# Order of work at five changes of stage in a one-core decoder layer: final scaling of the first token half, the mixer's second weights, the delta rule outputs' loads, the decays' product, the state banks

## The chip, the core and the metric

The kernel runs on one core of a Trainium2 chip. TensorE (PE in the rows) multiplies, VectorE (DVE), ScalarE (ACT) and GpSimd (POOL) work on tiles, and SyncE (SP) issues the transfers between device memory and the core's memory. Each engine takes its own instructions in the order in which they were written into its program. The metric is the time of one execution in microseconds (us).

## The reference: one layer of two feed-forward blocks around a mixer

1024 tokens of width 1024 pass through one layer: half a SwiGLU block (hidden width 2816), a mixer that runs a gated delta rule (8 heads) and a Mamba-2 state-space scan (16 heads) on one combined projection, another half SwiGLU block, and a last RMS norm. All is float32.

```python
def rms_norm(x, w):
    xf = x.astype(jnp.float32)
    y = xf * lax.rsqrt(jnp.mean(xf * xf, axis=-1, keepdims=True) + EPS)
    return (y * w.astype(jnp.float32)).astype(x.dtype)

def swiglu(h, w_gate, w_up, w_down):
    a = jnp.einsum("bld,df->blf", h, w_gate)
    b = jnp.einsum("bld,df->blf", h, w_up)
    return jnp.einsum("blf,fd->bld", jax.nn.silu(a) * b, w_down)
...
def hybrid_mixer(h, w_in, ...):
    proj = jnp.einsum("bld,de->ble", h, w_in).astype(jnp.float32)
    ...
    o = gated_delta_rule(q, k, v, g, beta)          # 8 heads of 128
    o = rms_norm(o, gdn_norm_w) * jax.nn.silu(gdn_z.reshape(bsz, seqlen, GDN_HEADS, GDN_HEAD_DIM))
    ...
    y = ssd_scan(xs, dt, a_neg, b, c)               # 16 heads of 64, 2 groups
    y = y + xs * ssm_d[:, None]
    y = y.reshape(bsz, seqlen, SSM_W) * jax.nn.silu(ssm_z)
    ...
    mixed = jnp.concatenate([o_gdn, o_ssm], axis=-1).astype(h.dtype)
    return jnp.einsum("ble,ed->bld", mixed, w_out)

def reference(x, ...):
    x = x + 0.5 * swiglu(rms_norm(x, ffn1_norm[i]), ffn1_w_gate[i], ffn1_w_up[i], ffn1_w_down[i])
    x = x + hybrid_mixer(rms_norm(x, mix_norm[i]), w_in[i], ...)
    x = x + 0.5 * swiglu(rms_norm(x, ffn2_norm[i]), ffn2_w_gate[i], ffn2_w_up[i], ffn2_w_down[i])
    return rms_norm(x, final_norm)
```

## The kernel before

Each float32 operand is split into two parts, a rounded one and the rest: ACT casts (`A.copy`, the high part), and DVE subtracts the cast from the source (the low part). A product is then three matmuls of 128x128 by 128x512 (high by high, high by low, low by high; `mm3` and `product`). So every weight tile goes through a load (SP), a cast (ACT) and a subtraction (DVE) before TensorE can use it, and the order of these in the three queues decides when it is ready. Python code is written stage by stage; a scheduler places each stage's instructions by its own priorities, and within an engine the order is then fixed. `tc.issue_after(x)` keeps what is written under it behind the instruction x.

The stages in order: ffn1 (gate and up products, then the down products, each by a seven-product scheme on 512x512 blocks), the mixer's projections and the four units of the state-space scan (`un` 0 to 3), the eight delta-rule heads, the output projection with `w_out`, ffn2, and the final norm. The change touches five places where one stage hands over to the next.

**The mixer's first products (lines 629 to 660, 732).** The last down product of ffn1 finishes its four token blocks of the second half one by one. `norm_second` squares them, makes `rstd` and the scaled rows `xn` (one on ACT, L645, one on DVE, L646), and `norm_ht` lets TensorE transpose them (L196), eight times four blocks; ACT writes `hhi` (L213) and DVE `hlo` (L214). The projection weights come by `next_w`, which hands out a ready pair `whi`, `wlo` and starts the next: one load `wst`, two casts L136, two subtractions L137.

**The state-space units (lines 801 to 950).** A unit transposes its inputs four times into the two buffers of the PSUM tag `mx` (L844); DVE reads each bank twice, for `xdt` and `xe` (L849, eight instructions). `state()` makes seven of the running states: one product of `xe` and `bn` into the one bank of the tag `oo` (L858), four multiplications on ACT (L865), one addition on DVE that frees the bank (L867). `decays(b)` loads a broadcast row into `md`, and makes `cte` (one exponential on ACT, one product on DVE, L878) and `md` (a mask on POOL, eight exponentials on ACT, L884, one product with `cbt` on DVE, L886). Then the outputs come in two batches of 128x128 products (L899); a batch starts only when both of its `md` are made and its states are there:

```python
first = inter(1, 1, 0)
tc.add_manual_dep(first.ins, pairs[1][4].ins.name, ..., reason="one run of products")
```

**The delta rule's outputs (lines 955 to 975, 1243 to 1290).** Each head stores its output `vr` and its gate to device memory (`mix_scr`, `z_scr`). In the output projection `out_prep` takes a pair of heads: it loads `nat` (the outputs, 1 MB) and `zg` (the gates, two loads), both in the ring of weight tiles `wst`; TensorE transposes `nat` (L965), DVE scales by the gate (`hd`, L968), ACT and DVE split into `mtt` (L970, L971). There are four such preparations: two for the pairs of `n = 0`, two for those of `n = 1`. The loads of the weights `w_out` (`out_w`) use the ring too.

**The end of ffn2 (lines 438 to 510, 1309 to 1352).** The last of the seven down products (`m == 7`) has six steps, numbered 0 to 5 here; step 5 is half as wide. For each step `dn.prep` loads two weight blocks `wst` and the hidden rows `hraw`, DVE adds the blocks (L450), and ACT and DVE split both (`hid` and `wd`, L218 and L219). Steps 2 to 5 are multiplied bank by bank, so TensorE needs the weights of steps 2 to 5 within the first of four token blocks. After the sixth product (`m == 6`) the first token half is complete, and `finish_first` squares it (L164), makes `rstd` (eleven short DVE instructions) and scales the four blocks by `rstd` and the norm's weights (L1321), with a store behind each.

## Time and profile before

| | us |
|---|---|
| median of 3 runs (lowest to highest) | 2347.31 (2346.55 to 2348.21) |
| the profiled execution, its own time | 2346.0 |
| its span, first to last instruction | 2344.0 |
| TensorE busy | 2288.8 (98%) |
| VectorE busy | 1726.0 (74%) |
| ScalarE busy | 1100.7 (47%) |
| mean granted TensorE clock | 0.997 |

The span is read against TensorE's busy time: what is left, 55.2 us, are its idle stretches. A row of the timeline gives the start, the duration, engine, line, operation and tiles, and in square brackets the idle time of that engine before it with what ended it.

### The profile page before, as it was taken

What the parts mean: (1) busy time and instruction counts of PE and PEld (TensorE: products, weight loads), DVE (VectorE), ACT (ScalarE), POOL (GpSimd) and SP (SyncE); (2) the same over time, 40 slices, a digit from 0 to 9 for tenths busy, and PEclk for the clock granted to TensorE, in tenths of its full rate; (3) what the DMA queues carried; (4) which work ended last, traced back from release to release, by engine and by line L of the source; (5) the groups of instructions that cost most, each with busy time, mean ns of one, the idle gap of its engine ahead of it and who ended that gap; (6) DMA issues with size and microseconds to landing.
All of it is one profiled execution on the core that took longest, in us unless ns stands there. A gap on an engine that the chain in (4) does not pass through costs nothing.

```text
span 2344.0 us, 31560 instructions
## 1 busy us (share of the span) xinstructions
PE 2288.8 (98%) x11798; PEld 1873.4 (80%) x11798; DVE 1726.0 (74%) x3332; ACT 1100.7 (47%) x1996; POOL 52.8 (2%) x117
## 2 busy tenths in 40 slices
PE   6999999999999999999999999999999999999997
PEld 4788888888878878788888888787878888888886
DVE  7877777667765675668778878777697777766787
ACT  7433333343357775773455555422553333334334
POOL 0000000000000110000000000000000000000000
PEclk9999999999999999999999999999999999999999
DMA  2332333474652222232332222326222333329445
GB/s 110 108 113 95 108 103 113 160 289 130 220 179 74 90 90 60 68 93 64 82 82 73 80 82 65 109 66 255 90 86 97 108 108 111 108 92 343 147 155 196
DMA packets 220968, 281.33 MB, mean 120 GB/s; under 512 B 46906, under 2 KB 153591, under 8 KB 219791
## 3 DMA queue, kind: packets, MB, share of 16 engines
q1 hardware_dynamic: 220814, 279.33, 36.4%
q8 instruction: 92, 1.51, 0.3%
q14 instruction: 62, 0.50, 0.1%
HBM read 211.55 MB, written 67.73 MB: 119 GB/s over the span
## 4 chain that ended last, share of the span: by engine, by line
PE 79%; DVE 7%; issue 6%; ACT 5%; DMA 2%; POOL 1%; SPq 0%; DVEq 0%; POOLq 0%; ACTq 0%
PE ps_pj L121 8%; PE ps_pj L123 8%; PE ps_pj L122 8%; PE ps_pj L314 6%; PE ps_pj L313 6%; PE ps_pj L315 6%; PE ps_mx L313 3%; PE ps_mx L314 3%; PE ps_mx L315 3%; PE ps_pj L472 2%; PE ps_pj L473 2%; PE ps_pj L471 2%; PE ps_oo L313 2%; PE ps_oo L314 2%; PE ps_oo L315 2%
## 5 line engine op out<-in xcount | busy, mean ns | idle before, releaser
L121 PE MATMUL ps_pj<-hhi,whi 128*128 128x512 f32 x832 | 335.5, 403 | 0.0
L123 PE MATMUL ps_pj<-hhi,wlo 128*128 128x512 f32 x832 | 333.2, 400 | 0.0
L122 PE MATMUL ps_pj<-hlo,whi 128*128 128x512 f32 x832 | 332.9, 400 | 0.0
L314 PE MATMUL ps_pj<-bl,ah 128*128 128x512 f32 x704 | 274.9, 391 | 1.9 <-DVE bl L219 1.9
L313 PE MATMUL ps_pj<-bh,ah 128*128 128x512 f32 x704 | 274.6, 391 | 1.9 <-ACT sg L373 0.9
L315 PE MATMUL ps_pj<-bh,al 128*128 128x512 f32 x704 | 274.1, 390 | 0.0
L121 PEld LDWEIGHTS ps_pj<-hhi,whi 128*128 128x128 f32 x832 | 157.0, 189 | 28.8 <-issue 0.7
L123 PEld LDWEIGHTS ps_pj<-hhi,wlo 128*128 128x128 f32 x832 | 157.0, 189 | 28.5
L122 PEld LDWEIGHTS ps_pj<-hlo,whi 128*128 128x128 f32 x832 | 157.0, 189 | 27.7
L313 PEld LDWEIGHTS ps_pj<-bh,ah 128*128 128x128 f32 x704 | 131.8, 188 | 32.7 <-ACT bh L218 2.5
L218 ACT CAST ah<-wst 128x512 fp32r<-128x512 f32 x88 | 54.7, 623 | 219.2 <-PE ps_oo L314 137.8
L314 PEld LDWEIGHTS ps_pj<-bl,ah 128*128 128x128 f32 x704 | 132.2, 188 | 31.4 <-DVE bl L219 4.7
L315 PEld LDWEIGHTS ps_pj<-bh,al 128*128 128x128 f32 x704 | 132.2, 188 | 27.2
L218 ACT CAST hid<-hraw 128x1024 fp32r<-128x1024 f32 (+1 forms) x84 | 82.1, 980 | 146.5 <-PE ps_oo L473 55.8
L292 DVE TENSOR_TENSOR as<-wst 128x512 f32<-128x512 f32 x220 | 145.0, 684 | 1.6 <-DMA wst<-in_ffn_w_up_dram 1.5
L219 DVE TENSOR_TENSOR al<-as,ah 128x512 fp32r<-128x512 f32 x220 | 140.2, 684 | 4.3 <-ACT ah L218 4.3
L313 PE MATMUL ps_mx<-bh,ah 128*128 128x512 f32 x352 | 137.5, 393 | 0.9 <-ACT bh L218 0.7
L314 PE MATMUL ps_mx<-bl,ah 128*128 128x512 f32 x352 | 138.0, 392 | 0.2 <-DVE bl L219 0.2
L315 PE MATMUL ps_mx<-bh,al 128*128 128x512 f32 x352 | 137.4, 390 | 0.0
L218 ACT CAST ah<-as 128x512 fp32r<-128x512 f32 x220 | 124.2, 617 | 14.3 <-DVE as L292 14.1
L219 DVE TENSOR_TENSOR hid<-hraw,hid 128x1024 fp32r<-128x1024 f32 x84 | 95.0, 1132 | 35.3 <-ACT hid L218 34.6
L219 DVE TENSOR_TENSOR al<-wst,ah 128x512 fp32r<-128x512 f32 x88 | 60.6, 690 | 74.0 <-ACT ah L218 73.9
(412 smaller groups left out, 5094.3 us busy)
## 6 DMA issues: line engine op xcount, KB each, us to landing
hraw<-hid_scr SPq DMA_DIRECT2D x70, 512.0 KB, 4.0
hid_scr<-hs SPq DMA_DIRECT2D x110, 256.0 KB, 2.2
wst<-in_ffn_w_down_dram SPq DMA_DIRECT2D x50, 512.0 KB, 4.3
wst<-in_ffn_w_gate_dram SPq DMA_DIRECT2D x22, 1024.0 KB, 5.4
wst<-in_ffn_w_up_dram SPq DMA_DIRECT2D x22, 1024.0 KB, 5.2
wst<-in_w_in_dram SPq DMA_DIRECT2D x36, 512.0 KB, 5.3
hid_scr<-sg SPq DMA_DIRECT2D x44, 256.0 KB, 2.0
keep<-in_ffn_w_down_dram SPq DMA_DIRECT2D x20, 512.0 KB, 7.6
```

The costliest lines, as they stand in the source:

```text
L121: T.matmul(o, lhsT=wh, rhs=mh, start=first, stop=False)
L122: T.matmul(o, lhsT=wh, rhs=ml, start=False, stop=False)
L123: T.matmul(o, lhsT=wl, rhs=mh, start=False, stop=last)
L218: A.copy(out=hi, in_=src)
L219: V.tensor_tensor(out=lo, in0=src, in1=hi.bitcast(F32), op=ALU.subtract)
L292: V.tensor_tensor(out=t, in0=v[0], in1=v[1], op=v[2])
L313: T.matmul(bank, lhsT=wh[:, k], rhs=bh[:, k], start=a, stop=False, skip_group_check=True)
L314: T.matmul(bank, lhsT=wh[:, k], rhs=bl[:, k], start=False, stop=False, skip_group_check=True)
L315: T.matmul(bank, lhsT=wl[:, k], rhs=bh[:, k], start=False, stop=z, skip_group_check=True)
L471: T.matmul(bank, lhsT=hh, rhs=wh, start=first and k == 0, stop=False, skip_group_check=True)
L472: T.matmul(bank, lhsT=hh, rhs=wl, start=False, stop=False, skip_group_check=True)
L473: m = T.matmul(bank, lhsT=hl, rhs=wh, start=False, stop=last and k == n - 1, skip_group_check=True)
```

## The change

Five edits, all on the order of work or on where it is buffered; no arithmetic is added or removed.

1. `finish_first` keeps the squares and `rstd`; the four scalings with their stores, and the parts of the second token half that were called `early`, move into `between()`. It is handed to `down_all` as the hook that runs when the last step of `m == 7` has been prepared.
2. `norm_ht` returns its last ACT instruction, and the mixer's first `next_w()` (the second weights) is placed behind it with `issue_after`.
3. `out_prep` is cut in two, `out_load` and the rest. `nat` and `zg` leave the ring `wst` for a pool `natp` of their own with one buffer each. The first pair's loads are written two blocks into `n == 1`, the second pair's behind the first preparation, ahead of the weights `out_w`.
4. The product of `md` with `cbt` is placed behind the unit's last `xe`.
5. `state()` uses the tags `oo` and `mx` in turn.

```diff
--- before.py
+++ after.py
@@ -210,9 +210,10 @@
         ts = slice(half * 512, (half + 1) * 512)
         for k in range(NK):
             pt = transposed(xns, k)
-            A.mul(out=hsl(hhi, k, ts), in_=pt, mul=wcol[:, k:k + 1])
+            m = A.mul(out=hsl(hhi, k, ts), in_=pt, mul=wcol[:, k:k + 1])
             V.scalar_tensor_tensor(out=hsl(hlo, k, ts), in0=pt, scalar=wcol[:, k:k + 1],
                                    in1=hsl(hhi, k, ts).bitcast(F32), op0=ALU.mult, op1=ALU.subtract)
+        return m
 
     def split(hi, lo, src):
         A.copy(out=hi, in_=src)
@@ -646,7 +647,7 @@
             V.tensor_scalar(out=xn[:, 1], in0=xt[4 + i], scalar1=r[:, 1:2], scalar2=None, op0=ALU.mult)
             xns.extend((xn[:, 0], xn[:, 1]))
             if i == 3:
-                norm_ht(1, xns, nrm[1], *h2)
+                h2.append(norm_ht(1, xns, nrm[1], *h2))
 
         def before_last():
             load_gates_w()
@@ -654,7 +655,7 @@
 
         with tc.tile_pool(name="dtmp0", bufs=1, reuse_waits="tile") as dtmp:
             down_all(dtmp, xt, x_v, dn, [before_last], norm_first, lambda i: square(i, 1), norm_second)
-        hhi, hlo = h2
+        hhi, hlo, last_h = h2
 
     cm = ExitStack()
     gp = cm.enter_context(tc.tile_pool(name="gates", bufs=1, reuse_waits="tile"))
@@ -729,7 +730,9 @@
                 T.matmul(p[0:64], lhsT=gw[:, k], rhs=hsl(hlo, k, ts), start=False, stop=(k == NK - 1))
             A.copy(out=gsb[:, ts], in_=p[0:64])
 
-        wa = next_w()
+
+        with tc.issue_after(last_h.ins):
+            wa = next_w()
         bt = gp.tile([P, L], F32, name="bt", tag="xst", bufs=2)
         conv_silu(s1, wa, 0, cw_s, 8, bt, bias=cb_s[:, 8:9], between=gate_proj)
         pt = psum("mx")
@@ -846,7 +849,8 @@
             ptv = pt.rearrange("p (i h c) -> p i h c", i=2, h=4)
             for name, lst, sc in (("xdt", xdts, bc2(dtn, b0)), ("xe", xes, bc2(dxe, b0))):
                 t = s1.tile([P, 2, 256], F32, name=name, tag=name, bufs=4)
-                V.tensor_tensor(out=t.rearrange("p i (h c) -> p i h c", h=4), in0=ptv, in1=sc, op=ALU.mult)
+                last_x = V.tensor_tensor(out=t.rearrange("p i (h c) -> p i h c", h=4), in0=ptv, in1=sc,
+                                         op=ALU.mult)
                 lst.append(t)
 
 
@@ -854,7 +858,7 @@
 
         def state():
             b = len(sts) - 1
-            p3 = psum("oo")
+            p3 = psum(("oo", "mx")[b % 2])
             T.matmul(p3[:, 0:256], lhsT=bn[:, b], rhs=xes[b // 2][:, b % 2], start=True, stop=True)
             sn = s2p.tile([P, 256], F32, name="sn2", bufs=6)
             if b == 0:
@@ -883,8 +887,9 @@
                 for j in range(2):
                     A.activation(out=md[:, i, j], in_=md[:, i, j], func=AF.Exp,
                                  bias=ngc[:, b + j, hh:hh + 1])
-            made = V.tensor_tensor(out=md, in0=md,
-                                   in1=cbt[:, b:b + 2].unsqueeze(1).to_broadcast([P, 4, 2, P]), op=ALU.mult)
+            with tc.issue_after(last_x.ins):
+                made = V.tensor_tensor(out=md, in0=md, in1=cbt[:, b:b + 2].unsqueeze(1)
+                                       .to_broadcast([P, 4, 2, P]), op=ALU.mult)
             return md, cte, made
 
 
@@ -952,12 +957,15 @@
 
     pools = []
 
-    def out_prep(grp, mh, ml):
-        nat = wp.tile([P, NB, 256], F32, name="nat", tag="wst")
+    def out_load(grp):
+        nat = natp.tile([P, NB, 256], F32, name="nat")
         nc.sync.dma_start(out=nat, in_=mix_scr[grp])
-        zg = wp.tile([P, 2, L], F32, name="zg", tag="wst")
+        zg = natp.tile([P, 2, L], F32, name="zg")
         for j in range(2):
             nc.sync.dma_start(out=zg[:, j], in_=z_scr[2 * grp + j])
+        return nat, zg
+
+    def out_prep(nat, zg, mh, ml):
         for j in range(2):
             for half in range(2):
                 pt = psum("mx")
@@ -995,6 +1003,8 @@
         ready0.append(group_prep(0))
 
 
+    cn = ExitStack()
+    natp = cn.enter_context(tc.tile_pool(name="natp", bufs=1, side="right", reuse_waits="tile"))
     with ExitStack() as cg:
         g1 = cg.enter_context(tc.tile_pool(name="gdn1", bufs=1, reuse_waits="tile"))
         g2 = cg.enter_context(tc.tile_pool(name="gdn2", bufs=2, reuse_waits="tile"))
@@ -1240,13 +1250,13 @@
         else:
             V.scalar_tensor_tensor(out=o, in0=p, scalar=r, in1=o, op0=ALU.mult, op1=ALU.add)
 
-    def pair_prep(n, g, ms):
+    def pair_prep(n, g, ms, loaded=None):
 
         if n == 0:
             m = mtt[2 * g:2 * g + 2]
         else:
             m = [hbp[0].tile([P, 2, L], F32R, name="mt2", tag=f"b{2 * g + i}") for i in range(2)]
-        out_prep(2 * n + g, *m)
+        out_prep(*(loaded or out_load(2 * n + g)), *m)
         ms.append(m)
 
     def pair_tile(b, dh, w, ms, o):
@@ -1269,12 +1279,15 @@
 
             if b == 2 and n < 3:
                 ready = group_prep(n + 1)
+                if n == 1:
+                    loaded = out_load(0)
             elif b == 2:
+                pair_prep(0, 0, ms[0], loaded)
+                loaded = out_load(1)
                 wa = out_w(0, 0)
-                pair_prep(0, 0, ms[0])
             for dh in range(2):
                 group_tile(n, b, dh, *cur)
-    pair_prep(0, 1, ms[0])
+    pair_prep(0, 1, ms[0], loaded)
     wb = out_w(0, 1)
     for b in range(NB):
         nc.sync.dma_start(out=xt2[b], in_=x_scr[:, b])
@@ -1302,6 +1315,7 @@
     x1 = normalise(1, npool, xt2, jtag="h7")
     b_second(npool, x0, x1, nrm[2], H)
     c2.close()
+    cn.close()
 
 
     dn = gate_up_phase(1, npool, H, ffn2_w_gate[0], ffn2_w_up[0], ffn2_w_down[0], raws, ops)
@@ -1317,10 +1331,7 @@
         nc.sync.dma_start(out=wrow, in_=final_norm.partition_broadcast(P))
         junk = npool.tile([P, D], BF16, name="junk", tag="q")
         r = rms_stats(npool, xt2, 0, 4, junk)
-        for b in range(4):
-            V.scalar_tensor_tensor(out=xt2[b], in0=xt2[b], scalar=r[:, b:b + 1], in1=wrow,
-                                   op0=ALU.mult, op1=ALU.mult)
-            nc.sync.dma_start(out=out_v[:, b], in_=xt2[b])
+        rows.append(r)
 
     def part(i, dh):
 
@@ -1329,11 +1340,16 @@
         A.activation(out=junk, in_=xt2[4 + i][:, ds], func=AF.Square, accum_out=ss[:, 4 * dh + i:4 * dh + i + 1])
         V.tensor_tensor(out=xw[i // 2][:, i % 2, ds], in0=xt2[4 + i][:, ds], in1=rows[0][:, ds], op=ALU.mult)
 
-    def early(i):
-        part(i, 1)
-        if i == 3:
-            V.tensor_scalar(out=ss[:, 4:8], in0=ss[:, 4:8], scalar1=1.0 / D, scalar2=EPS,
-                            op0=ALU.mult, op1=ALU.add)
+    def between():
+
+        for b in range(4):
+            V.scalar_tensor_tensor(out=xt2[b], in0=xt2[b], scalar=rows[1][:, b:b + 1], in1=rows[0],
+                                   op0=ALU.mult, op1=ALU.mult)
+            nc.sync.dma_start(out=out_v[:, b], in_=xt2[b])
+        for i in range(4):
+            part(i, 1)
+        V.tensor_scalar(out=ss[:, 4:8], in0=ss[:, 4:8], scalar1=1.0 / D, scalar2=EPS,
+                        op0=ALU.mult, op1=ALU.add)
 
     def finish(i):
         part(i, 0)
@@ -1349,7 +1365,7 @@
             nc.sync.dma_start(out=out_v[:, 4 + i, dh * 512:(dh + 1) * 512], in_=o[:, dh * 512:(dh + 1) * 512])
 
     with tc.tile_pool(name="dtmp1", bufs=1, reuse_waits="tile") as dtmp:
-        down_all(dtmp, xt2, x_scr, dn, [], finish_first, early, finish)
+        down_all(dtmp, xt2, x_scr, dn, [between], finish_first, lambda i: None, finish)
 
 
 NAMES = ["x", "ffn1_norm", "ffn1_w_gate", "ffn1_w_up", "ffn1_w_down", "mix_norm", "w_in",
```

On ACT, at the mixer's first products (`xn`: scaled rows of the second token half, `whi`: high part of the mixer's second weights, `hhi`: high part of the transposed rows). Before:

```order
L631 ACTIVATE junk,ss_3721<-xtb 128x512 x3
L645 ACTIVATE xn<-xtb,rstd 128x1024
L136 CAST whi<-wst 128x8x128
L645 ACTIVATE xn<-xtb,rstd 128x1024
L136 CAST whi<-wst 128x8x128
L213 ACTIVATE hhi<-ps_sc,cols 128x512 x4
```

After:

```order
L632 ACTIVATE junk,ss_3721<-xtb 128x512 x3
L646 ACTIVATE xn<-xtb,rstd 128x1024 x2
L213 ACTIVATE hhi<-ps_sc,cols 128x512 x5
L770 ACT_TABLE_LOAD
L770 ACTIVATE alog<-alog 128x24
L213 ACTIVATE hhi<-ps_sc,cols 128x512 x3
L136 CAST whi<-wst 128x8x128 x2
```

The two casts of the weights stood around the second `xn`; they now stand behind the eighth `hhi`, and the two `xn` follow each other.

On DVE, at the start of unit 1's outputs (`md`: decays times `cbt`, `xdt` and `xe`: scaled inputs that free the transposes' banks, `sn`: states, `wlo`: low part of projection weights). Before:

```order
L886 TENSOR_TENSOR md<-md,cbt 128x1024
L878 TENSOR_TENSOR cte<-cte,ct 128x1024
L886 TENSOR_TENSOR md<-md,cbt 128x1024
L849 TENSOR_TENSOR xdt<-ps_mx,dtn 128x512
L849 TENSOR_TENSOR xe<-ps_mx,dxe 128x512
L849 TENSOR_TENSOR xdt<-ps_mx,dtn 128x512
L849 TENSOR_TENSOR xe<-ps_mx,dxe 128x512
L849 TENSOR_TENSOR xdt<-ps_mx,dtn 128x512
L849 TENSOR_TENSOR xe<-ps_mx,dxe 128x512
L849 TENSOR_TENSOR xdt<-ps_mx,dtn 128x512
L849 TENSOR_TENSOR xe<-ps_mx,dxe 128x512
L861 COPY sn_6436<-ps_oo 128x256
```

After:

```order
L882 TENSOR_TENSOR cte<-cte,ct 128x1024
L852 TENSOR_TENSOR xdt<-ps_mx,dtn 128x512
L852 TENSOR_TENSOR xe<-ps_mx,dxe 128x512
L852 TENSOR_TENSOR xdt<-ps_mx,dtn 128x512
L852 TENSOR_TENSOR xe<-ps_mx,dxe 128x512
L852 TENSOR_TENSOR xdt<-ps_mx,dtn 128x512
L852 TENSOR_TENSOR xe<-ps_mx,dxe 128x512
L852 TENSOR_TENSOR xdt<-ps_mx,dtn 128x512
L852 TENSOR_TENSOR xe<-ps_mx,dxe 128x512
L865 COPY sn_6436<-ps_oo 128x256
L891 TENSOR_TENSOR md<-md,cbt 128x1024 x2
L871 TENSOR_TENSOR sn_6440<-ps_mx,sn_6440 128x256
```

Both products of `md` stood ahead of the first `xdt`; they now stand behind the first state, and the second state reads a bank of `mx`.

On DVE, in the last down product of ffn2 (`wst`: sum of two weight blocks, `wd`: their low part, `hid`: low part of the hidden rows, 128x1024 in steps 3 and 4, 128x512 in step 5). Before, from the four scalings through the weights of step 3 (the first `wd`), step 4 and step 5 to the first addition of the second token half:

```order
L1321 SCALAR_TENSOR_TENSOR xt2b<-xt2b,rstd,wrow 128x1024 x4
L219 TENSOR_TENSOR wd<-wst,wd 128x1024
L450 TENSOR_TENSOR wst<-wst 128x1024
L219 TENSOR_TENSOR hid<-hraw,hid 128x1024
L219 TENSOR_TENSOR hid<-hraw,hid 128x512
L219 TENSOR_TENSOR wd<-wst,wd 128x1024
L450 TENSOR_TENSOR wst<-wst 128x512
L219 TENSOR_TENSOR wd<-wst,wd 128x512
L477 SCALAR_TENSOR_TENSOR xt2b<-ps_pj,xt2b 128x512
```

After, beginning behind the split of step 3's weights with the sum of step 4's:

```order
L451 TENSOR_TENSOR wst<-wst 128x1024
L117 TENSOR_TENSOR rs_t<-rs_t,rstd 128x4
L1351 TENSOR_SCALAR ss_18312<-ss_18312 128x4
L118 SCALAR_TENSOR_TENSOR rstd<-rs_t,rstd 128x4
L1346 SCALAR_TENSOR_TENSOR xt2b<-xt2b,rstd,wrow 128x1024
L220 TENSOR_TENSOR hid<-hraw,hid 128x1024
L220 TENSOR_TENSOR wd<-wst,wd 128x1024
L451 TENSOR_TENSOR wst<-wst 128x512
L1346 SCALAR_TENSOR_TENSOR xt2b<-xt2b,rstd,wrow 128x1024
L220 TENSOR_TENSOR wd<-wst,wd 128x512
L1346 SCALAR_TENSOR_TENSOR xt2b<-xt2b,rstd,wrow 128x1024 x2
L478 SCALAR_TENSOR_TENSOR xt2b<-ps_pj,xt2b 128x512
```

The four scalings stood in one run ahead of the split of step 3's weights; they now stand behind it, one ahead of step 4's split, one ahead of step 5's, and two behind that.

## Rows read from the trace of the kernel before

**Rows 1.** The page's first part: busy us, share and instructions of each engine.

```profile
PE 2288.8 (98%) x11798; PEld 1873.4 (80%) x11798; DVE 1726.0 (74%) x3332; ACT 1100.7 (47%) x1996; POOL 52.8 (2%) x117
```

**Rows 2.** Waits of PE: line, waited for; us in all, times, longest.

```profile
PE ps_pj L472 <- DVE wd L219: 5.1, 4, 3.2
PE ps_mx L844 <- DVE xe L849: 3.6, 2, 1.8
PE ps_oo L858 <- DVE sn L867: 2.9, 4, 0.8
```

**Rows 3.** Windows: us, busy of PE, PEld, DVE, ACT, POOL; granted clock, DMA share, GB/s.

```profile
686.80:690.20 3.40, 3.40 (x11) 2.55 (x10) 2.13 (x3) 0.72 (x2) 0.00 (x0) 0.50 0.50 121
1594.80:1598.20 3.40, 3.40 (x12) 2.66 (x11) 3.34 (x6) 1.96 (x4) 0.00 (x0) 0.50 0.29 91
2304.05:2311.53 7.48, 7.48 (x35) 6.20 (x33) 6.40 (x17) 5.06 (x9) 0.00 (x0) 1.00 0.50 164
2315.00:2318.40 3.40, 3.00 (x6) 1.77 (x6) 3.40 (x5) 1.05 (x1) 0.00 (x0) 0.50 0.96 314
```

**Rows 4.** Timeline of ACT, DVE, PE at the mixer's first products.

```profile
683.33 1.04 ACT L136 CAST whi<-wst 128x1024 fp32r<-128x1024 f32 x1 [3.65 <-DMA wst<-in_w_in_dram]
684.27 1.15 ACT L645 ACTIVATE xn<-xtb,rstd 128x1024 f32<-128x1024 f32 x1
...
681.04 0.75 DVE L646 TENSOR_SCALAR xn<-xtb,rstd 128x1024 f32<-128x1024 f32 x1
...
685.48 0.65 PE L196 MATMUL ps_sc<-ident,xn 128*128 128x128 f32 x4 [2.79 <-ACT xn L645]
```

**Rows 5.** Timeline of DVE and PE in state-space unit 1.

```profile
822.22 1.23 DVE L886 TENSOR_TENSOR md<-md,cbt 128x1024 f32<-128x1024 f32 x1 [6.88 <-ACT md L884]
...
833.32 0.42 DVE L867 TENSOR_TENSOR sn<-ps_oo,sn 128x256 f32<-128x256 f32 x1 [2.15 <-ACT sn L865]
...
847.22 1.23 DVE L886 TENSOR_TENSOR md<-md,cbt 128x1024 f32<-128x1024 f32 x1 [0.82 <-ACT md L884]
...
824.79 0.63 PE L844 MATMUL ps_mx<-ident,xs 128*128 128x128 f32 x4 [1.82 <-DVE xe L849]
```

**Rows 6.** Timeline of SP, DVE, PE at the second output preparation.

```profile
1585.96 0.32 SPq L957 DMA_DIRECT2D nat<-mix_scr  x1
...
1593.51 1.41 DVE L968 SCALAR_TENSOR_TENSOR hd<-ps_mx,cols,zg 128x512 f32<-128x512 f32 x2 [3.82 <-DMA zg<-z_scr]
...
1592.28 1.06 PE L965 MATMUL ps_mx<-ident,nat 128*128 128x128 f32 x8 [1.58 <-DMA nat<-mix_scr]
1594.32 0.74 PE L965 MATMUL ps_mx<-ident,nat 128*128 128x128 f32 x4 [0.97 <-DVE hd L968]
```

**Rows 7.** Timeline of PE in the last down product.

```profile
2311.53 0.39 PE L471 MATMUL ps_pj<-wd,hid 128*128 128x512 f32 x1
2315.12 0.79 PE L472 MATMUL ps_pj<-wd,hid 128*128 128x512 f32 x1 [3.21 <-DVE wd L219]
...
2319.12 0.50 PE L472 MATMUL ps_pj<-wd,hid 128*128 128x512 f32 x1 [1.00 <-DVE wd L219]
...
2321.21 0.50 PE L472 MATMUL ps_pj<-wd,hid 128*128 128x512 f32 x1 [0.22 <-DVE wd L219]
```

**Rows 8.** Timeline of DVE and ACT in the last down product.

```profile
2300.98 1.22 DVE L219 TENSOR_TENSOR wd<-wst,wd 128x1024 fp32r<-128x1024 f32 x1
...
2304.85 0.17 DVE L166 TENSOR_SCALAR ssv<-ss 128x4 f32<-128x4 f32 x1 [1.52 <-ACT junk L164]
...
2309.06 4.87 DVE L1321 SCALAR_TENSOR_TENSOR xt2b<-xt2b,rstd,wrow 128x1024 f32<-128x1024 f32 x4
2313.85 1.22 DVE L219 TENSOR_TENSOR wd<-wst,wd 128x1024 fp32r<-128x1024 f32 x1
...
2316.23 1.05 ACT L218 CAST wd<-wst 128x1024 fp32r<-128x1024 f32 x1 [3.97 <-DVE wst L450]
```

**Rows 9.** The page's sixth part: transfers, count, KB each, us to landing.

```profile
wst<-in_ffn_w_down_dram SPq DMA_DIRECT2D x50, 512.0 KB, 4.3
```

## Prediction

> **What bounds the kernel now.** The first part of the page comes first: TensorE is busy for 2288.8 us [rows 1], and the span is 2344.0 us, so all that an order of work can win is in 55.2 us of idle time, plus what a lowered clock costs. No step here takes a product away. The table of what TensorE waits for comes next. Three of its rows belong to the places that are edited: the weights of the down product, 5.1 us, of which 0.6 lie elsewhere, as the three waits of the last product add up to 3.21 + 1.00 + 0.22 = 4.43 [rows 2, 7]; the `mx` banks behind `xe`, 3.6 us in two waits; the `oo` bank behind `sn`, 2.9 us in four [rows 2]. The timeline adds 2.79 us before the transposes of `xn` [rows 4] and 1.58 and 0.97 us at the second output preparation [rows 6]. The third view is the granted clock: three stretches of 3.40 us stand at 0.50, which is 1.2 GHz, and each begins right behind one of these waits, 686.8 behind the 2.79, 1594.8 behind the 1.58 and 0.97, 2315.0 behind the 3.21 [rows 3, 4, 6, 7]. At half speed 3.40 us of products give 1.7 us of work at full speed, so each such stretch costs 1.7 us. The waits of 1.8 us in the state-space units have no such stretch behind them. In all the places hold 4.43 + 3.6 + 2.9 + 2.79 + 2.55 + 3 x 1.7 = 21.4 us, 0.9% of the time. That is the ceiling.
>
> **The mixer's second weights.** ACT runs in order. It had the cast of `whi` ahead of the second ACT `xn`, and the cast waited for its load to 683.33; `xn` ran at 684.27 and TensorE's transposes at 685.48 [rows 4]. The same `rstd` was ready at 681.04, where DVE made its own `xn` [rows 4]. With the casts behind the last `hhi`, `xn` can start at 681.04 and end at 681.04 + 1.15 = 682.19. TensorE stood there from 685.48 - 2.79 = 682.69 [rows 4], so the wait goes whole, and with it the stretch at 0.50: 2.79 + 1.7 = 4.49. What is late next: the casts and the two DVE subtractions behind them now run after eight evictions. These weights serve the projection behind the gates and the first B and C columns, so many products lie between. The load behind them starts later as its ring slot is freed later; I take 0.5 for a small wait in the chain of eight evictions, whose banks ACT and DVE free in turn. **Gain 4.0, bounds 2.5 and 4.8** (the lower one if one wait of half the old length, 1.4, comes back without the slow clock and 0.6 behind it; the upper adds 0.3 of earlier evictions).
>
> **The decays' product and the state banks.** In unit 1 DVE waited 6.88 us, to 822.22, for the last exponential of `md`, though the transposes to be read stood ready; the bank came free late and TensorE waited 1.82 us [rows 5]. Behind `xe`, the product no longer holds DVE: the eight reads take as long as before, but begin about 2 us sooner, so TensorE's third transposes find their bank. That happens in units 1 and 3: 3.6 us [rows 2]. The four waits on the single `oo` bank, 2.9 us, of which 0.3 at the longest is jitter in my reading, go where the next state has another bank. What takes their place: the two products of `md`, 1.23 us each [rows 5], now stand between the first state and the second. By my walk through DVE's new order in unit 1, the third state, which the first batch needs, ends at 831.9 instead of 833.32 + 0.42 = 833.74 [rows 5], and TensorE comes for it at about 832.0; that is nearly no margin. For the second batch the last `md` product ended at 847.22 + 1.23 = 848.45 [rows 5]; ACT reaches its exponentials 1.8 to 2 us sooner, so 846.3 to 846.6, where TensorE comes at about 846.2 to 846.8. So of 6.5 I take 5.0, losing 0.2 in each of eight batches. **Gain 5.0, bounds 1.5 and 6.5** (the lower one: only the 3.6 is gained and 0.26 per batch lost).
>
> **The delta rule's outputs.** Only the first pair's loads come early. The second pair's share one buffer with them: `nat` waits for the first preparation's transposes, which is what released it at 1585.96 before too [rows 6], so the transfer lands about where it did, at 1592.28 [rows 6], perhaps 0.9 us sooner as the first eight transposes no longer alternate with products. In front of the second `hd`, DVE now has four splits of `w_out`, 1.16 to 1.22 us each by the nearest row, a split of the same 128x1024 shape [rows 8]: 4.7 us, against a gap of 3.82 that DVE waited there for `zg` to 1593.51 [rows 6]. So `hd` comes at 1593.5 to 1594.5, up to 1.0 late, and TensorE's wait before it grows by as much. The splits came behind, under products that TensorE had anyway, so moving them wins nothing. In the heads, two more transfers per place go through SP's queue, ahead of loads that have microseconds of cover. **Loss 0.5, bounds a gain of 2.0** (an earlier `nat` with `zg`, and one wait less) **and a loss of 3.0** (`hd` 1.0 late, and SP's moved loads 2.0 late at one place).
>
> **The final scaling.** Before, the four scalings, 4.87 us, stood ahead of step 3's split, which ended at 2315.07; TensorE needed it at 2311.53 + 0.23 and waited 3.21 [rows 7, 8]. Without that wait and its slow stretch the last product ends 4.43 + 1.7 = 6.1 us sooner. Now the order on DVE: `rstd` can start when the fourth square is done, at 2304.85 before [rows 8] and about 1.0 later with a cast between (1.05 [rows 8]), 2305.8. Five of its short instructions (0.2 each, by the 0.17 of [rows 8] and the issue) and two splits of 1.22 [rows 8] bring step 3's weights to 2309.4, well ahead of 2311.5. Step 4: its load is issued when step 2's split is done, 2300.98 + 1.22 before [rows 8], now behind one more split, 2303.4, and lands 4.3 us later [rows 9], 2307.7 to 2308.5, no limit. Then DVE has the hidden rows of step 5 (0.7), the sum of step 4 (1.2), short ones (0.8), one scaling (1.22), the hidden rows (1.22) and the split (1.22) to do: 2309.4 + 6.4 = 2315.8, against TensorE's need at 2311.53 + 7 x 0.227 = 2313.1 (7.48 us at full clock hold 33 products and parts of two more at the ends, 0.227 each [rows 3]). Stall: 2.4 to 2.7. Step 5 adds sum (0.7), scaling (1.22) and split (0.7): 2.6, against 6 products, 1.4: stall 1.2. Together 3.6 to 3.9. Two waits of 2.5 and 1.2 so near each other look like the pair 1.58 and 0.97, behind which the clock fell [rows 3, 6]; then 1.7 remains as well, and the gain is 6.1 - 3.7 - 1.7 = 0.7. Without it, 2.4. The two scalings behind the last split hold the first addition by 2.4 us, but a block of 21 products lasts 21 x 0.227 = 4.8 and DVE's work per block 4.1, so that is made up before the end. I take the middle, **gain 1.5, bounds 0 and 6.1.**
>
> In what ends a wait and lowers the clock the rows show only which waits were followed by 0.50. The Trainium skill, TensorE: Matmul & The Clock Gate, section "What's actually happening", says that the throttled state is the default and that activity releases it. The trace agrees in that each of the three stretches follows idle time. By that rule alone nearly every wait left could bring the 0.50 back, and the last product would then gain 0.7; the 1.8 us waits of the units, at full clock, speak against so wide a reading.
>
> **The sum.** 4.0 + 5.0 - 0.5 + 1.5 = 10.0. The profiled execution took 2346.0 (its span and 2.0 around it), so 2336.0; the median of the runs is 1.3 above it, 2347.3, so the forecast is **2337.3 us**, 0.43% less. All other stages keep their order.
>
> **The rivals.**
> (1) All waits of the five places go: 6.1 + 4.5 + 6.5 = 17, **2330.3**. For it: each edit aims at the engine row that ended a wait. Against: step 4's chain above is too long by 2 us, and the second `nat` has no second buffer.
> (2) The waits move: the third state ends where it did because the products of `md` (2.5 us) delay it, so the units win only their lower bound, 1.5; the outputs lose 1.0 and the last product gains nothing. Then 4.0 + 1.5 - 1.0 = 4.5 less, **2342.8**. For it: the margin of 0.1 us in the first batch, and DVE's strict order. Against: TensorE also has states placed earlier.
> (3) Slower, by one mechanism: the two `md` products, now between the first and second state, stand on the path of every batch. If TensorE waits for them whole, 2.46 us in each of eight batches, that is 19.7 lost against 6.5 won, and with the other places' 5.0 won the sum is 8.2 more: **2355.5**. It decides from (6.5 + 5.0 + 4.7) / 8 = 2.0 us a batch. Against it: only the first batch's states follow those products, and the eight reads in front of them begin 2 us sooner.
>
> **How the numbers follow.** About 0.2%, 4.7 us, can be told from no change: faster is under 2342.6, slower over 2352.0. Chances: forecast 0.61 (2333 to 2342 by its bounds), rival 1 0.12, rival 2 0.21, rival 3 0.06. The range reaches from rival 1 to a little beyond rival 2, 2330 to 2345. Faster: forecast and rival 1, 0.73; same: rival 2, 0.21; slower 0.06.
>
> **What would show it right or wrong.** After: no wait for `xn` and no 0.50 near 687; no wait for `xe` and none for `sn` over 0.4; a wait for `nat` and `hd` near 1590 of 2 to 4 us in all, with its 0.50; in the last product two waits for `wd` of about 2.5 and 1.2 with no wait at step 3. The forecast is wrong if TensorE shows new waits before L904 (the batches) of over 0.5 each, if the second preparation costs more than 5 us, or if the last product has no wait or one over 4.

## The result

The changed kernel takes 2330.94 us (median of 6 runs, 2327.78 to 2333.58), the kernel before 2346.93 on the same chip (6 runs, 2345.69 to 2348.21): a ratio of 0.9932 [0.9919, 0.9944], or 16.0 us less. The forecast was 10.0 less. The time lies inside the range, 0.9 above its lower end, next to rival 1 (2330.3), and below the 2333 to 2342 that the forecast gave as its own bounds.

The profiled execution took 2327.78, with a span of 2326.0, the fastest of the six. The page's first part stands against [rows 1]:

```profile
PE 2282.8 (98%) x11798; PEld 1870.1 (80%) x11798; DVE 1724.9 (74%) x3332; ACT 1099.8 (47%) x1996; POOL 49.4 (2%) x117
```

TensorE's idle time falls from 55.2 to 43.2 us. Its busy time falls by 6.0 with the same 11798 instructions; some 4.6 of that lie in the three stretches of the table below that had a part at half clock. Next, what TensorE waits for (us in all, times, longest), after, against [rows 2]:

```profile
PE ps_mx L973 <- DVE hd L976: 3.0, 1, 3.0
...
PE ps_pj L473 <- DVE wd L220: 2.5, 4, 1.2
...
PE ps_sc L196 <- ACT xn L646: 0.5, 2, 0.3
```

The rows of `xe` and `sn` are gone, that of `wd` is halved, and one wait of 3.0 for `hd` stands at the second output preparation. The granted clock (the column behind POOL's, as in [rows 3]) at the three places that had 0.50:

```profile
682.70:686.10 3.40, 3.40 (x23) 2.91 (x21) 1.66 (x3) 2.23 (x4) 0.00 (x0) 1.00 0.09 21
1584.00:1587.40 3.40, 3.40 (x16) 2.79 (x15) 3.38 (x6) 0.64 (x2) 0.00 (x0) 1.00 1.03 417
2301.50:2304.90 3.40, 2.76 (x12) 1.83 (x11) 3.40 (x4) 0.48 (x1) 0.00 (x0) 1.00 0.39 154
```

How far TensorE is ahead at the same instruction of both traces shows where the time went (to about 0.2, as neighbouring products can change places):

| TensorE instruction | before | after | ahead | won since |
|---|---|---|---|---|
| first transposes of `xn` | 679.73 | 679.81 | -0.1 | |
| unit 0's first transposes | 763.83 | 760.66 | 3.2 | mixer's weights 3.2 |
| behind the last unit | 1001.87 | 991.17 | 10.7 | units 7.5 |
| late in the heads | 1505.39 | 1493.56 | 11.8 | 1.1, only the first early loads |
| behind the second preparation | 1614.91 | 1600.84 | 14.1 | outputs 2.2 |
| early in ffn2 | 1693.48 | 1679.66 | 13.8 | -0.3, the last two preparations |
| end of the last down product | 2335.89 | 2317.84 | 18.05 | final scaling 4.2 |

**Mixer.** TensorE's timeline, after, against [rows 4] (between the two, rows left out):

```profile
679.81 0.66 PE L196 MATMUL ps_sc<-ident,xn 128*128 128x128 f32 x4 [0.17 <-ACT xn L646]
...
682.38 0.66 PE L196 MATMUL ps_sc<-ident,xn 128*128 128x128 f32 x4 [0.30 <-ACT xn L646]
...
694.95 0.50 PE L121 MATMUL ps_pj<-hhi,whi 128*128 128x512 f32 x1 [0.38 <-ACT gsb L731]
```

The wait of 2.79 has become three of 0.85 together; the first of them, 0.17, ends at the first landmark of the table. From there to unit 0 TensorE's idle time falls from 2.81 to 0.71, so 2.1 of the 3.2 won are idle time; 1.1 are left for the clock.

**Unit 1.** DVE, then TensorE, after, against [rows 5]:

```profile
817.23 0.69 DVE L852 TENSOR_TENSOR xdt<-ps_mx,dtn 128x512 f32<-128x512 f32 x1 [5.61 <-PE ps_mx L847]
...
822.35 2.35 DVE L891 TENSOR_TENSOR md<-md,cbt 128x1024 f32<-128x1024 f32 x2
824.62 0.41 DVE L871 TENSOR_TENSOR sn<-ps_mx,sn 128x256 f32<-128x256 f32 x1
...
816.59 1.03 PE L847 MATMUL ps_mx<-ident,xs 128*128 128x128 f32 x8
...
818.66 0.63 PE L847 MATMUL ps_mx<-ident,xs 128*128 128x128 f32 x4
```

DVE now waits for TensorE's transposes, not for ACT; the third transposes find their bank free, and the two `md` products stand between the states without holding TensorE.

**Second output preparation.** DVE and TensorE, after, against [rows 6]:

```profile
1576.58 2.35 DVE L137 TENSOR_TENSOR wlo<-wst,whi 128x1024 fp32r<-128x1024 f32 x2
1578.85 2.35 DVE L220 TENSOR_TENSOR wld<-wst,whd 128x1024 fp32r<-128x1024 f32 x2
1581.12 2.24 DVE L976 SCALAR_TENSOR_TENSOR hd<-ps_mx,cols,zg 128x512 f32<-128x512 f32 x3
...
1577.84 1.06 PE L973 MATMUL ps_mx<-ident,nat 128*128 128x128 f32 x8
1581.92 0.66 PE L973 MATMUL ps_mx<-ident,nat 128*128 128x128 f32 x4 [3.01 <-DVE hd L976]
```

`nat` is in time, and so is `zg` (no idle time before `hd`). The four splits of `w_out` stand ahead of `hd`, and TensorE waits for them. Between the landmarks around this stage (the row of 2.2 in the table) TensorE's idle time falls by 0.6 and its busy time by 1.6, as no part of it is at 0.50 now. One of the waits that became shorter is for `xa`, ahead of these rows: 1.45 before, 0.67 after.

**Last down product.** DVE, then TensorE, after, against [rows 7, 8]:

```profile
2291.47 0.17 DVE L166 TENSOR_SCALAR ssv<-ss 128x4 f32<-128x4 f32 x1 [0.72 <-ACT junk L164]
...
2293.76 1.22 DVE L220 TENSOR_TENSOR wd<-wst,wd 128x1024 fp32r<-128x1024 f32 x1
...
2294.97 0.69 DVE L220 TENSOR_TENSOR hid<-hraw,hid 128x512 fp32r<-128x512 f32 x1
...
2295.64 1.22 DVE L451 TENSOR_TENSOR wst<-wst 128x1024 f32<-128x1024 f32 x1
...
2297.17 1.28 DVE L1346 SCALAR_TENSOR_TENSOR xt2b<-xt2b,rstd,wrow 128x1024 f32<-128x1024 f32 x1
2298.37 1.22 DVE L220 TENSOR_TENSOR hid<-hraw,hid 128x1024 fp32r<-128x1024 f32 x1
2299.51 1.22 DVE L220 TENSOR_TENSOR wd<-wst,wd 128x1024 fp32r<-128x1024 f32 x1
2300.64 0.68 DVE L451 TENSOR_TENSOR wst<-wst 128x512 f32<-128x512 f32 x1
...
2300.78 0.50 PE L473 MATMUL ps_pj<-wd,hid 128*128 128x512 f32 x1 [1.23 <-DVE wd L220]
...
2303.18 0.50 PE L473 MATMUL ps_pj<-wd,hid 128*128 128x512 f32 x1 [0.64 <-DVE wd L220]
```

Step 3's split is done at 2294.98 and TensorE doesn't wait there. Steps 4 and 5 cost 1.23 and 0.64, and the clock stays at 1.00.

### The profile page after: what moved, and what is told of

It is laid out like the page before. It is cut to its first block, busy times and chain, and to the rows that moved or that the text cites. A ratio compares the mean times of both kernels' runs of the same rounds, so it can differ in the third digit from the quotient of the medians.

```text
span 2326.0 us, 31552 instructions
## 1 busy us (share of the span) xinstructions
PE 2282.8 (98%) x11798; PEld 1870.1 (80%) x11798; DVE 1724.9 (74%) x3332; ACT 1099.8 (47%) x1996; POOL 49.4 (2%) x117
## 5 line engine op out<-in xcount | busy, mean ns | idle before, releaser
L220 DVE TENSOR_TENSOR hid<-hraw,hid 128x1024 fp32r<-128x1024 f32 (+1 forms) x84 | 95.0, 1131 | 35.0 <-ACT hid L219 34.5
```

Of the source, the lines that this page charges most:

```text
L220: V.tensor_tensor(out=lo, in0=src, in1=hi.bitcast(F32), op=ALU.subtract)
```

## The experiments

All runs had five or six rounds against the kernel before on the same chip; medians are in us. The kernel before has medians of 2346.8 (runs `again` to no_md), 2347.3 (no_banks to splits_late), 2345.8 (zg_two and the two of the scalings) and 2345.6 (best) there, so that differences between groups are also given by the ratios. One edit is undone in each of the first; the diffs show the core, `-` being the changed kernel.

**again.** The changed kernel once more.

> The changed kernel once more, to see what differs between its own executions. Its six runs lay from 2327.8 to 2333.6 us where those of the kernel before lay within 2.5, and its profiled one showed no stretch at a granted clock of 0.50 in the three places that had one before. Theory A (the waits that are left are sometimes followed by 0.50): another profiled execution shows one or two stretches of 3.4 us at 0.50, behind the wait of 3.0 us for hd or behind the two waits in the last product, and lies 1.7 us higher for each; median 2330 to 2332. Theory B (no such stretch is left, the spread is in the transfers): no 0.50 again, and the times differ by waits for loads.

2330.91 (2329.69 to 2332.17), ratio 0.9931 [0.9917, 0.9944]. TensorE at the second preparation:

```profile
1582.89 1.12 PE L973 MATMUL ps_mx<-ident,nat 128*128 128x128 f32 x4 [3.11 <-DVE hd L976]
```

Three windows, the first of them from within this wait (granted clock third from the end):

```profile
1581.90:1585.30 3.40, 2.41 (x10) 2.23 (x11) 2.85 (x5) 1.71 (x3) 0.00 (x0) 0.50 1.04 423
1585.30:1588.70 3.40, 3.40 (x9) 2.63 (x9) 1.96 (x4) 0.77 (x2) 0.00 (x0) 0.51 1.03 411
1588.70:1592.10 3.40, 3.40 (x17) 2.77 (x16) 2.89 (x5) 0.00 (x0) 0.00 (x0) 1.00 1.01 416
```

The same wait is here accompanied by 6.8 us at 0.50, where the first trace had none: theory A held. From unit 0's first transposes to the last product this run takes 1559.40 against 1557.18. So some 2.2 us between runs of one program go with whether the clock falls at this wait, and the 18.05 of the first trace is 2 above the medians' 16.0.

**no_scaling.** Edit 1 undone.

```diff
-        down_all(dtmp, xt2, x_scr, dn, [between], finish_first, lambda i: None, finish)
+        down_all(dtmp, xt2, x_scr, dn, [], finish_first, early, finish)
```

> Only the first edit is undone: the four scalings stand ahead of step 3's weights again, the other four edits stay. Theory A (each edit is worth what its own place shows in the traces): the last product ends 4.2 to 6.1 us later in its own frame, 2335 to 2337, with the wait of 3.2 us at step 3 back and 0.50 behind it. Theory C (VectorE's whole work in the last 40 us sets the end, whatever its order): within 1.5 us of the changed kernel, 2330 to 2332.5, as the later end of the products is made up by an earlier start of the last additions.

2336.66 (2335.49 to 2337.16), 0.9955 [0.9943, 0.9968]: 5.7 slower than the changed kernel, as theory A had it; the ranges of the two don't meet. TensorE in the last down product:

```profile
2304.74 0.80 PE L473 MATMUL ps_pj<-wd,hid 128*128 128x512 f32 x1 [3.22 <-DVE wd L220]
...
2308.75 0.79 PE L473 MATMUL ps_pj<-wd,hid 128*128 128x512 f32 x1 [0.99 <-DVE wd L220]
```

The windows there:

```profile
2304.00:2309.00 5.00, 3.27 (x7) 2.03 (x8) 4.75 (x6) 1.05 (x1) 0.00 (x0) 0.50 0.76 265
2309.00:2314.00 5.00, 5.00 (x12) 3.86 (x13) 2.72 (x4) 1.33 (x3) 0.00 (x0) 0.50 0.00 0
```

The two long waits of before return to a hundredth, but 0.50 lasts 10 us and not 3.4, so the edit is worth more here than the 4.2 of the table.

**no_weights.** Edit 2 undone.

```diff
-        with tc.issue_after(last_h.ins):
-            wa = next_w()
+        wa = next_w()
```

> Only the second edit is undone: the casts of the mixer's second weights stand ahead of the second xn again. Theory A: the wait of 2.8 us for xn and the 3.4 us at 0.50 behind it come back, 3.2 to 4.5 us, 2334 to 2335.5. Rival (the wait for xn only moves a wait that comes later in the gates): under 1.5 us, 2330 to 2332.5.

2332.85 (2329.8 to 2334.57), 0.9939 [0.9927, 0.9952]: 1.9 slower, with intervals that overlap. The trace says more:

```profile
686.38 1.07 PE L196 MATMUL ps_sc<-ident,xn 128*128 128x128 f32 x4 [2.80 <-ACT xn L646]
```

From the first transposes of `xn` to those of unit 0 it takes 84.11, as before (84.10), against 80.85 and 81.32 in the two traces of the changed kernel and 80.91 to 81.68 in those of the other runs that have the edit. The edit is worth 2.4 to 3.3 by these traces, 1.9 by medians that can't tell it from 3 (theory A had 3.2 to 4.5).

**no_md, no_banks, no_md_banks.** Edit 4, edit 5 and both undone.

```diff
-            with tc.issue_after(last_x.ins):
-                made = V.tensor_tensor(out=md, in0=md, ...)
+            made = V.tensor_tensor(out=md, in0=md, ...)
...
-            p3 = psum(("oo", "mx")[b % 2])
+            p3 = psum("oo")
```

> Only the fourth edit is undone: the product of md with cbt stands ahead of xdt and xe again, the state banks still alternate. Theory A (the two edits in the units stand apart, as their waits did): the two waits of 1.8 us for xe come back in units 1 and 3, 3.6 us or a little more, 2334 to 2335.5. Rival (with two banks the states wait too as the second bank comes from the transposes' pair): 5 us or more, over 2336.

> Only the fifth edit is undone: all states use the one bank of oo again, the product of md stays behind the last xe. With the fourth edit undone the changed kernel lost nothing (2331.0 against 2330.9), as the order of ACT's exponentials had moved with the banks. Theory D (the two edits of the units cover for each other at xe; the banks alone bring the waits for sn): no wait for xe, four waits of 0.7 us for sn come back, 3 us in all, 2333.5 to 2334.5. Rival (the banks carry the whole gain of the units): 6 to 7.5 us, 2337 to 2338.5.

> The fourth and the fifth edit are undone together: the units stand as in the kernel before, the other three edits stay. Theory D: the waits of 1.8 us for xe in units 1 and 3 and the four for sn come back, 6.5 to 7.5 us in all, 2337.5 to 2338.5; that is more than the two edits undone one by one add up to (0 and 3 us). Rival (the gain of the units is made up elsewhere): under 4 us.

no_md 2330.98 (2329.74 to 2331.89), 0.9931 [0.9919, 0.9944]; no_banks 2330.79 (2329.52 to 2333.41), 0.9932 [0.9920, 0.9945]; no_md_banks 2338.98 (2337.84 to 2340.24), 0.9966 [0.9954, 0.9978]. So the two together are worth 8.1, and each of them alone gives nearly all of it: the expectation that each undoes its own waits fell. The traces agree. From unit 0's first transposes to the products behind the last unit it takes 238.04 before and 238.15 in no_md_banks, 230.51 in the changed kernel, 230.86 in no_md and 232.32 in no_banks, the last two with a stretch at 0.50 near 856 (see the end). With both undone the waits of [rows 2] return:

```profile
PE ps_mx L847 <- DVE xe L852: 3.7, 2, 1.8
PE ps_oo L862 <- DVE sn L871: 2.9, 4, 0.8
```

Neither row is in either single run. In no_md the product of `md` is back in its old place, but ACT has its exponentials done in time (ACT, then DVE, of no_md, unit 1):

```profile
810.61 1.87 ACT L888 ACTIVATE md<-md,ngc 128x128 f32<-128x128 f32 x6
...
812.57 1.23 DVE L890 TENSOR_TENSOR md<-md,cbt 128x1024 f32<-128x1024 f32 x1 [6.97 <-ACT md L888]
817.88 0.69 DVE L852 TENSOR_TENSOR xdt<-ps_mx,dtn 128x512 f32<-128x512 f32 x1 [4.08 <-PE ps_mx L847]
```

DVE waited as long as in [rows 5], 6.97, but 5 us before the transposes came, not on top of them. In no_md_banks, which differs from no_md in the banks alone, ACT's last exponentials of this `md` end at 819.11, here at 812.48: with the other banks the scheduler placed them earlier. No run moves the exponentials alone. In no_banks `xdt` starts with the transposes at 817.54, and the sixth state's bank is free at 836.45, 0.3 before TensorE comes for it, where ACT and DVE stand further ahead of it. For `sn` this is read from the rows and not tried, and why the scheduler chose these orders was not followed up.

**no_loads.** Edit 3 undone: `nat` and `zg` back in the ring, loaded where they are used.

```diff
-        nat = natp.tile([P, NB, 256], F32, name="nat")
+        nat = wp.tile([P, NB, 256], F32, name="nat", tag="wst")
```

> Only the third edit is undone: nat and zg use the weights' ring again, all preparations load late. Theory E (the early load only changed the cause of the wait at the second preparation, from the transfer to VectorE's splits of the output weights, 3.0 us against 1.6 and 1.0 before): within 1.5 us either way, 2329.5 to 2332.5, with the waits for nat and hd back. Rival (it is worth what the landmarks of the two profiles show between the last head and ffn2, 2.0 us, or more): 2333 to 2334.

2331.02 (2329.86 to 2331.19), 0.9931 [0.9918, 0.9943]: no difference. TensorE's waits around the preparations of this run are 0.24, 0.42, 1.46 (`nat`), 0.96 (`hd`) and 0.19, in all 3.27, against the 3.01 of the changed kernel; the wait for `xa` ahead of them is 1.45 again, against 0.67. Edit 3 swaps one cause for another. From behind the last unit to the last down product no_loads takes 1328.30 with the clock at 1.00 throughout, the changed kernel 1326.67 so and 1328.86 in `again`, with its 6.8 us at 0.50: what the early loads win, the longer wait can lose again by the clock.

**splits_late.** In the changed kernel the splits of `w_out` go behind the second preparation's last `hd`.

```diff
+        behind = tc.issue_after(last_hd[7].ins) if (pr, dh) in ((0, 1), (1, 1)) else nullcontext()
+        with behind:
+            return out_split(pr, dh, st)
```

> The changed kernel with one more order: the splits (cast and subtraction) of the two output weights that stood ahead of the second preparation's hd are placed behind its last hd; the loads stay where they are. Theory E (VectorE's 4.7 us of splits ahead of hd set the wait of 3.0 us): the wait falls to 1 to 2 us, then set by the landing of zg, and the stretch at 0.50 behind it goes in most executions; 1.5 to 4 us less than the changed kernel, 2327 to 2329.5. Rival (zg lands no earlier than the splits end): no change, 2330 to 2332; or the splits then hold the first additions of the next pairs, and it is slower.

2331.36 (2329.59 to 2332.58), 0.9931 [0.9919, 0.9944]. DVE, then TensorE:

```profile
1582.47 1.41 DVE L976 SCALAR_TENSOR_TENSOR hd<-ps_mx,cols,zg 128x512 f32<-128x512 f32 x2 [3.00 <-DMA zg<-z_scr]
...
1583.28 0.66 PE L973 MATMUL ps_mx<-ident,nat 128*128 128x128 f32 x4 [1.36 <-DVE hd L976]
...
1590.65 0.63 PE L121 MATMUL ps_pj<-whi,mtt 128*128 128x512 f32 x1 [1.87 <-DVE xa L1277]
```

The wait for `hd` did fall to 1.36, as theory E had it, with 0.26 for `nat`, but the gain is missing, as the rival had it: the splits mostly fill a gap that `zg` leaves anyway (DVE waits 3.00 for it), and behind `hd` they hold the additions that free TensorE's banks (1.87).

**zg_two.** The pool holds two early `zg` and `nat` goes back to the ring, so that the second `zg` waits for nothing.

```diff
-    natp = cn.enter_context(tc.tile_pool(name="natp", bufs=1, side="right", reuse_waits="tile"))
+    natp = cn.enter_context(tc.tile_pool(name="natp", bufs=2, side="right", reuse_waits="tile"))
...
-                    loaded = out_load(0)
+                    zgs = [zg_load(g) for g in range(2)]
```

> The changed kernel with another third edit: the pool natp holds two zg and no nat; both pairs' zg load early, nat goes back to the weights' ring. The third edit as it stands was worth nothing (2331.0 without it against 2330.9), and moving VectorE's splits behind hd only brought out the next cause: hd then waited 3.0 us for zg, whose load waits for the one buffer. Theory E (the single zg buffer sets the wait at the second preparation; the splits only hide it): with two buffers hd follows the transposes, the wait of 3.0 us and the stretch at 0.50 behind it go; 3 to 5 us less than the changed kernel, 2326 to 2328. Rival (nat in the ring comes late instead): a wait for nat of 1.5 us or more and no change, 2330 to 2332.

2330.73 (2328.88 to 2332.26), 0.9935 [0.9922, 0.9947]: the expected gain is missing. TensorE, in the order of time:

```profile
1587.29 0.50 PE L121 MATMUL ps_pj<-whi,mtt 128*128 128x512 f32 x1 [1.77 <-DVE xa L1275]
...
1618.87 0.50 PE L121 MATMUL ps_pj<-whi,mtt 128*128 128x512 f32 x1 [1.40 <-DVE xt L1275]
```

The waits for `nat` and `hd` are gone (0.23 left), and 3.17 come back further on, for additions that stand behind the splits. DVE is busy for 18.59 of the 20 us from 1573.3; in the changed kernel it is 19.80 of 20 from 1570.5, before it was 14.40 of 20 from 1583.5. The wait of 1.77 is followed by 3.4 us at 0.50. What is short here seems to be DVE's time, not a load; the last run tries that.

**scaling_last and scaling_pool.** In the changed kernel the four scalings stand behind the last split; or they leave DVE (ACT multiplies by `rstd`, GpSimd by the weights).

```diff
+        with tc.issue_after(dn.last.ins):
             for b in range(4):
...
-            V.scalar_tensor_tensor(out=xt2[b], in0=xt2[b], scalar=rows[1][:, b:b + 1], in1=rows[0], ...)
+            A.mul(out=xt2[b], in_=xt2[b], mul=rows[1][:, b:b + 1])
+            G.tensor_tensor(out=xt2[b], in0=xt2[b], in1=rows[0], op=ALU.mult)
```

> The changed kernel with all four scalings behind step 5's split on VectorE, where now one stands ahead of step 4's split and one ahead of step 5's. Undoing the first edit cost 5.7 us. Theory F (a scaling ahead of a split that TensorE waits for costs its time; behind the splits the slack of VectorE, 4.1 of 4.8 us a block, takes it up): the waits of 1.2 and 0.6 us go, 1.5 to 2 us less than the changed kernel, 2329. Theory C (VectorE is full from the squares to the end, so only its work counts): TensorE's waits go, but the first addition comes 2.4 us later and the last blocks catch up only in part: within 0.7 us, 2330 to 2331.5.

> The changed kernel with the four scalings taken off VectorE: ScalarE multiplies by rstd (128x1024, 1.04 us each), GpSimd by the weights of the norm, the store follows. Theory C (VectorE's work in the last 30 us sets the end): 4.9 us of VectorE go, the waits at steps 4 and 5 go, 2 to 4 us less than the changed kernel, 2327 to 2329. Rival (GpSimd is slow enough, or holds VectorE up enough, that the stores come last): the end waits for the last store of the first token half, and it is as long or longer.

scaling_last 2329.16 (2327.58 to 2331.55), 0.9932 [0.9918, 0.9945]: the two waits fall to 0.59 and 0.23, 1.05 less, too little to be told by the ratio, which is that of the changed kernel; theories F and C stay undecided. scaling_pool 2334.8 (2334.23 to 2335.45), 0.9952 [0.9940, 0.9965]: slower than the changed kernel by 3.9, by the ratios 4.7. GpSimd, DVE, ACT and TensorE of scaling_pool:

```profile
2302.05 10.82 POOL L1347 TENSOR_TENSOR xt2b<-xt2b,wrow 128x1024 f32<-128x1024 f32 x4 [787.05 <-ACT xt2b L1346]
...
2302.22 2.88 DVE L451 TENSOR_TENSOR wst<-wst 128x512 f32<-128x512 f32 x1
2305.78 2.08 DVE L220 TENSOR_TENSOR wd<-wst,wd 128x512 fp32r<-128x512 f32 x1 [0.68 <-ACT wd L219]
2309.17 0.69 DVE L478 SCALAR_TENSOR_TENSOR xt2b<-ps_pj,xt2b 128x512 f32<-128x512 f32 x1 [1.31 <-PE ps_pj L474]
...
2305.13 0.62 ACT L219 CAST wd<-wst 128x512 fp32r<-128x512 f32 x1 [1.14 <-DVE wst L451]
...
2305.80 0.61 PE L472 MATMUL ps_pj<-wd,hid 128*128 128x512 f32 x1 [2.02 <-ACT wd L219]
```

While GpSimd multiplies, DVE's addition of 128x512 takes 2.88 and its split 2.08, both 0.68 in the changed kernel; the addition that reads a PSUM bank keeps its 0.69. ACT's cast for step 5 waits 1.14 for that slow addition, TensorE waits 2.02 for the cast and then 1.50 for the split, and 6.8 us at 0.50 follow. The stores didn't come last, as the rival had it: GpSimd is done at 2312.87, the span ends at 2333.1. The Trainium skill, SBUF — State Buffer, section "Who interferes with whom", says that a VectorE instruction with two SBUF inputs contends with a GpSimd instruction that reads SBUF, and one with at most one SBUF input doesn't; these three rows of DVE agree. A fourth with two inputs there, `xw` at 2309.90, took only 0.74.

**best.** zg_two and scaling_last together, with the splits of `w_out` written into the loops: behind the fourth addition of the product before them.

```diff
+        added = pair_tile(b, 0, wa, ms[0], xa[b // 2][:, b % 2, 0:512])
+        if b == 3:
+            with tc.issue_after(added.ins):
+                wb = out_w(0, 1, wb)
```

> Three orders together: two early zg buffers as in the run before (its wait for hd was gone, but VectorE, busy without a break, then let two other waits of 1.8 and 1.4 us come out, behind the splits of the output weights), the four scalings behind step 5's split, and, new, the splits of the two output weights behind the fourth addition of the products before them, where TensorE does not need them for many products. Theory G (in the output projection VectorE's splits, wherever they stand among the preparations, are what makes TensorE wait): without them there the waits of this stage fall from 3 to 5 us to under 2, and its stretch at 0.50 goes: 2324 to 2327, 4 to 7 us less than the changed kernel. Rival (VectorE's work of that stage as a whole is the bound): the wait only moves once more, 2328 to 2331, of which the scalings bring 1.7 at most.

2325.13 (2324.61 to 2327.34), 0.9911 [0.9898, 0.9925], against 2345.61 for the kernel before: 5.8 below the changed kernel's median, and the two ranges don't meet, but on a chip where the kernel before is faster by 1.3. By the ratios it is 4.9, with intervals that overlap by 0.0006. TensorE at the second preparation:

```profile
1574.81 0.63 PE L976 MATMUL ps_mx<-ident,nat 128*128 128x128 f32 x4 [0.23 <-DVE hd L979]
...
1584.99 0.50 PE L121 MATMUL ps_pj<-whi,mtt 128*128 128x512 f32 x1 [1.14 <-ACT mtt L981]
...
1587.78 0.51 PE L121 MATMUL ps_pj<-whi,mtt 128*128 128x512 f32 x1 [0.21 <-DVE xa L1279]
```

1.58 in all against 3.01, and the clock stays at 1.00 from 1580 to 1590. From behind the last unit to the last down product it takes 1324.17, in scaling_last 1325.53, in the first trace of the changed kernel 1326.67 (the clock at 1.00 in all three) and in `again` 1328.86. So theory G held, though part of the gain may be that of the scalings. The second `zg` buffer alone and later splits alone gave nothing; these splits without the second `zg` buffer were not run, so that both are needed isn't shown.

## Why the prediction was right, and where its sizes were off

The four costs of undoing (5.7 + 1.9 + 8.1 + 0.1) add up to 15.8 of the 16.0, so the terms can be held against them one by one. That the sum comes out so near is in part luck: each ratio has an interval of 0.0013 either way, 3 us, and of the four only 5.7 and 8.1 belong to runs whose range doesn't meet the changed kernel's.

| term | forecast | by undoing | between the traces |
|---|---|---|---|
| mixer's weights | 4.0 | 1.9 | 3.2 |
| units (edits 4 and 5) | 5.0 | 8.1 | 7.5 |
| outputs' loads | -0.5 | 0.1 | 2.2 |
| final scaling | 1.5 | 5.7 | 4.2 |

- **Mixer's weights.** The mechanism held: no wait of 2.79, no 0.50 near 687. The allowance of 0.5 for new waits was a little too small (0.7 behind the first landmark), and the clock gave back 1.1, not 1.7.
- **Units.** The step that failed is the loss of 0.2 in each of eight batches for the two `md` products. TensorE has no such wait; in all units only one of 0.29 is left. The gain is even above the 6.5 of the two waits, by 1.0 between the traces and 1.6 by undoing. Between the traces this rest is not idle time but busy time of TensorE, 231.2 against 230.2 at a clock of 1.00 in both; what shortened it was not found. That either edit would do alone was not foreseen: the text took each wait as caused by the one thing that ended it, while at `xe` either edit was enough: the fourth takes the product out of the reads' way, and with the fifth alone ACT's exponentials came early enough for the old place (no_md). Rival 3 and the main part of rival 2 rested on these products and fall.
- **Outputs' loads.** The step on `hd` was right: it came late by the four splits, and the wait went from 2.55 to 3.01. By the medians the loads bought nothing. Of the 2.2 between the first traces 1.6 are the 0.50 that is missing in one of them; `again` has it, as have six of the nine traces with this wait.
- **Final scaling.** The step that failed is the chain from step 3's split to step 4's. It was summed with durations, 6.4; it took 5.75 (2294.98 to 2300.73). Back-to-back instructions of DVE start every 1.14 us with a duration of 1.22 (2298.37, 2299.51, 2300.64), and the short ones between long ones cost little: step 5's hidden rows, the sum and four short ones took 2.2 (2294.97 to 2297.17), where 0.7, 1.2 and 0.8 were put down. Step 3's split came 0.6 earlier too, 2294.98 against 2309.4 less the 13.8 by which ffn2 had moved: with that 13.8 the `rstd` chain, which begins at 2291.47, is 0.4 later than before (2304.85), where 1.0 had been allowed for a cast. So step 4's wait was 1.23 instead of 2.4 to 2.7 and step 5's 0.64 instead of 1.2. With no 0.50 behind them the gain is 6.1 - 1.87 = 4.2, as the table has it. The prediction's wide reading of the Trainium skill (TensorE: Matmul & The Clock Gate, section "What's actually happening": the throttled state is the default, activity releases it), by which nearly every wait left brings the 0.50 back, would have given 0.7. The traces speak against it: these two waits (1.23 to 1.53, and 0.64) left the clock at 1.00 in both traces of the changed kernel and in the seven others that have them.

The total was nearest to rival 1 without its mechanism: the waits of the outputs and of the last product did not go. Three of the four terms came out better than forecast by the traces, and the total fell below the forecast's own bounds; that it stayed within the wider range, by 0.9, was lucky. What held are the mechanisms of the mixer's weights, of `hd` and of step 3.

## What to carry to other kernels

Sum a chain on one engine with the pitch between starts of neighbouring rows, not with durations. Before an edit brings a transfer forward, look at how busy the engine is that consumes it: here the gap in front of `hd` was filled by four splits, and a gain showed only in the run that had both early transfers and better placed splits. Where a scheduler places the work, undo edits singly and together, since two of them can each be enough.
